# A list scheduler's order of 2,364 jobs replaced by one written plan, in a decoder trunk on one core

## The chip, the core and the metric

The kernel runs on one core of a Trainium2 chip. The metric is the device time of one execution in microseconds (us), as the median of several runs. One more execution was taken by the hardware profiler; all rows below come from that one.

## What is computed

One layer of a hybrid decoder trunk on 512 positions of width 1024, all in float32: a mixer with three branches, and a feed-forward part with a short convolution. `_causal_dwconv` is a convolution over positions, one filter for each channel; `y_c`, whose lines are left out, is attention with 4 heads to 256 memory rows.

```python
def _mixer(x, mem, ...):
    h = _rmsnorm(x, norm_mix_g)
    p_a, p_b, q, p_g = jnp.split(h @ w_in, IN_SPLITS, axis=-1)
    gb, gc, v = jnp.split(p_a, 3, axis=-1)
    y_a = (gb * _causal_dwconv(gc * v, conv_a_w)) @ w_a_out        # 3 taps
    u, ug = jnp.split(p_b, 2, axis=-1)
    u = _causal_dwconv(u * jax.nn.sigmoid(ug), conv_b_w) + conv_b_bias   # 31 taps
    y_b = jax.nn.silu(_layernorm(u, ln_b_g, ln_b_b)) @ w_b_out
    ...
    merged = g[:, :, 0] * y_a + g[:, :, 1] * y_b + g[:, :, 2] * y_c
    return merged @ w_o

def _conv_ffn(x, norm_ffn_g, w_up, conv_ffn_w, w_down):
    u = _causal_dwconv(_rmsnorm(x, norm_ffn_g) @ w_up, conv_ffn_w)   # 3 taps
    gt, up = jnp.split(u, 2, axis=-1)                                # 2 x 2816
    return (jax.nn.silu(gt) * up) @ w_down

# x = x + _mixer(...);  x = x + _conv_ffn(...);  out = _rmsnorm(x, norm_final_g)
```

## The kernel before, in words

**Products.** TensorE multiplies float32 in parts: every operand is split into a high part (an ACT cast, L649, `whi` for weights) and a low part (a DVE subtraction, L653, `wlo`), and each product is hi·hi, hi·lo and lo·hi. The large projections go further: four blocks of weights (2 x 2 blocks of 512 rows by 256 columns, 512 KB each) make a "quad" that is computed by seven products instead of eight, as in Strassen's method. A quad's products are named (quad, 1) to (quad, 7), for instance `(("up", 2), 6)`; each is 24 matmuls of 256 columns (`multiply`, L819). The operands that are sums of blocks are made in place by the DMA queue of POOL (GpSimd), which adds a block of weights onto a loaded tile (`more`, L773): for a quad q the jobs `("s5", q)`, `("s6", q)`, `("s7", q)`, `("s3", q)`. Plain loads of 512 KB go through SP's queue (L679): `("ld", (q, "u"))` and v, s, r. So a product in the feed-forward part hangs on a chain of load (SP), accumulate (POOL), cast `("wh", ...)` (ACT), subtraction `("wl", ...)` (DVE) and product (PE). The last projection (`pd`) and the merge use plain products of 512 or 256 columns (L600 to L602).

**Other work.** ACT and DVE read the products' banks (L864 and its neighbours on DVE, L848 to L885 on ACT), and DVE makes convolution taps (L1598), `z` = up times gate (L1969), its differences (`zs`, L606, and `zd`, L2170) and their low parts (`zl`, L2197). The last steps are sums of squares (`sr`, L2365), the root and the reciprocal (L2383, L2437), the scaling (`sa`, L2389, and `sv`, L2402) and the stores.

**What sets the order.** All work is put down as 2,364 jobs in the class `Jobs` (L244 to L467). A job has a name, an engine, a cost, a function that emits its instructions, the jobs that it comes after, the tiles that it takes and the tiles that it uses. A tile takes a slot of a ring: 17 `sb`, 6 `lf`, 8 banks of PSUM `ps`, 6 `wf` (the landing places of weights), 6 `tm`. `latest_starts` gives every job a due time from the order of the products and shifts it by a table for each kind of job (`LATER`); `run` then goes through a model of the machine, and again and again takes the job that can start first, by due time among equals, not earlier than `AHEAD` before its due time. It models the two DMA queues (`moved`, `transfer`, `SHARE`) and takes the slot that came free first. Each engine then executes its instructions in the order in which they were emitted. When the model lets a DMA of SP or POOL start later than its queue was free, `wait_for` makes it wait for the last instruction of PE, ACT or DVE that the model had ended by then:

```python
if start > free[e] + PACE and early:
    wait_for(self.tc, code[n_code], max(early, key=lambda d: d[0])[1])
```

The casts and subtractions write into a short ring of `whi` and `wlo` tiles: the cast for a product comes after the product `UNIT_BUFS` products earlier (in `split_job`).

Of the kernel before, what the change touches and what calls it, by code (L numbers as in the profile page):

```python
# [56 lines left out]
SOON = 8.0  # L57

SHARE = 0.39
# [18 lines left out]
LATER = {  # L78
    "ACT c3": -79.87, "ACT cf": -109.54, "ACT csq": -49.02, "ACT exp": -408.18,
# [3 lines left out]
    "ACT mg": -6.51, "ACT mgh a": -131.92, "ACT mgh b": -203.04, "ACT mgh c": -161.97,  # L83
    "ACT mgh d": -323.72, "ACT mgh e": -90.58, "ACT mgh f": 308.75, "ACT mgh g": -153.29,
    "ACT msq": 15.04, "ACT mu high": -0.01, "ACT oh": -226.41, "ACT pth": -176.82,
# [12 lines left out]
    "ACT table end": -197.25, "ACT table exp": 5.67, "ACT table gates": 1.59,  # L98
    "ACT table glu": -252.31, "ACT table last": -0.01, "ACT table silu": -28.73,
    "ACT table swish": -15.77, "ACT table v": -32.24, "ACT table x": -1.37, "ACT tap 0": -202.88,  # L100
    "ACT tap 1": 192.35, "ACT tap 2": 130.71, "ACT tap 3": 262.1, "ACT tp 0": 393.84,
# [9 lines left out]
    "ACT xroot": -17.08, "ACT xsq": 6.07, "ACT xsquare": -30.79, "ACT zh a": -613.81,  # L111
    "ACT zh b": -91.24, "ACT zh d": -69.92, "ACT zh e": -4.53, "ACT zh f": -126.12,
    "ACT zh g": -8.78, "DVE CV": -695.74, "DVE c3": -191.73, "DVE centre": 202.15,
    "DVE cf": 294.92, "DVE csum": -277.07, "DVE ends": -149.6, "DVE fl h b00": 0.11,
# [6 lines left out]
    "DVE low": 2.25, "DVE m fold": 28.63, "DVE m scale": 0.66, "DVE mg": -19.19,  # L121
    "DVE mgl a": -285.28, "DVE mgl b": 9.87, "DVE mgl c": 24.34, "DVE mgl d": -328.43,
# [111 lines left out]
def wait_for(tc, ins, other):  # L234
# [5 lines left out]
        reason="paced",  # L240
    )


class Jobs:  # L244

    def __init__(self, tc, rings):
# [2275 lines left out]
```

## Time and profile before

| | before |
|---|---|
| median of 3 runs | 895.22 us (895.15 to 895.43) |
| span of the profiled execution | 894.3 us |
| PE busy | 886.0 us, 99% of the span |
| DVE busy | 822.5 us, 92% |
| ACT busy | 677.8 us, 76% |
| POOL busy | 126.8 us, 14% |
| moved by DMA | 190.59 MB, 213 GB/s in the mean |

Times are in us from the start of the span; in a row of a timeline the first column is the start, the second the busy time, then engine, line, operation, output<-inputs, shapes, the number of instructions put together, and in brackets the idle time of the engine just before with what ended it. Matmuls overlap, so the distance from start to start says what one costs, not its busy time.

### The profile page before, as it was taken

What the parts mean: (1) busy time and instruction counts of PE and PEld (TensorE: products, weight loads), DVE (VectorE), ACT (ScalarE), POOL (GpSimd) and SP (SyncE); (2) the same over time, 40 slices, a digit from 0 to 9 for tenths busy, and PEclk for the clock granted to TensorE, in tenths of its full rate; (3) what the DMA queues carried; (4) which work ended last, traced back from release to release, by engine and by line L of the source; (5) the groups of instructions that cost most, each with busy time, mean ns of one, the idle gap of its engine ahead of it and who ended that gap; (6) DMA issues with size and microseconds to landing.
All of it is one profiled execution on the core that took longest, in us unless ns stands there. A gap on an engine that the chain in (4) does not pass through costs nothing.

```text
span 894.3 us, 16686 instructions
## 1 busy us (share of the span) xinstructions
PE 886.0 (99%) x6649; PEld 847.4 (95%) x6649; DVE 822.5 (92%) x928; ACT 677.8 (76%) x933; POOL 126.8 (14%) x153
## 2 busy tenths in 40 slices
PE   9999999999999999999999999999999999999997
PEld 8999999999989999999899988899999999998886
DVE  6997999999989999999897969898999889999997
ACT  7767989989987888787967753776766677875665
POOL 0021121111011121111100011021211121001220
PEclk9999999999999999999999999999999999999999
DMA  9999789767569997988856497499999877779992
GB/s 357 391 256 209 151 196 195 189 138 171 165 161 233 210 212 179 231 190 218 212 111 213 178 337 160 115 236 309 281 239 231 210 163 151 197 261 323 229 220 96
DMA packets 54221, 190.59 MB, mean 213 GB/s; under 512 B 6144, under 2 KB 6528, under 8 KB 54144
## 3 DMA queue, kind: packets, MB, share of 16 engines
q0 software_dynamic: 20880, 75.24, 47.0%
q1 hardware_dynamic: 32976, 114.02, 35.3%
q8 instruction: 52, 0.85, 0.4%
q10 hardware_dynamic: 288, 0.27, 0.1%
q14 instruction: 25, 0.20, 0.1%
HBM read 185.31 MB, written 4.19 MB: 212 GB/s over the span
## 4 chain that ended last, share of the span: by engine, by line
PE 93%; DVE 5%; issue 1%; ACT 0%; DVEq 0%
PE bank L819 57%; PE bank L601 6%; PE bank L602 6%; PE bank L600 6%; PE bank L1649 5%; PE bank L1651 5%; PE bank L1650 5%; PE bank L1153 2%; DVE wlo L653 2%; DVE zl L2197 1%; DVE upc L1598 1%; DVE gtc L1598 1%; PE bank L2014 0%; PE bank L1889 0%; PE bank L1393 0%
## 5 line engine op out<-in xcount | busy, mean ns | idle before, releaser
L653 DVE TENSOR_TENSOR wlo<-wf,whi 128x1024 fp32r<-128x1024 f32 x196 | 235.0, 1210 | 22.6 <-ACT whi L649 22.4
L649 ACT CAST whi<-wf 128x1024 fp32r<-128x1024 f32 x202 | 209.4, 1042 | 60.8 <-PE bank L819 18.8
L1465 ACT ACTIVATE tp<-u,pk 128x511 f32<-128x511 f32 (+22 forms) x184 | 118.8, 705 | 3.1 <-DVE acc L1472 2.5
L1472 DVE TENSOR_TENSOR acc<-acc,tp 128x1022 f32<-128x1022 f32 (+22 forms) x92 | 109.2, 1187 | 6.8 <-ACT tp L1465 5.1
L773 POOL DMA_DIRECT2D wf<-in_w_in x52 | 46.5, 914 | 231.8 <-DVE wlo L653 148.5
L819 PE MATMUL bank<-ft6h,wlo 128*128 128x256 f32 x232 | 64.0, 276 | 1.1 <-DVE wlo L653 1.1
L819 PE MATMUL bank<-fb10h,whi 128*128 128x256 f32 x232 | 64.0, 276 | 0.0
L819 PE MATMUL bank<-fb11h,whi 128*128 128x256 f32 x232 | 64.0, 276 | 0.0
L819 PE MATMUL bank<-ft5l,whi 128*128 128x256 f32 x232 | 63.9, 275 | 0.0
L819 PE MATMUL bank<-fb11h,wlo 128*128 128x256 f32 x232 | 63.9, 275 | 0.0
L819 PE MATMUL bank<-fb00h,whi 128*128 128x256 f32 x232 | 63.9, 275 | 0.0
L819 PE MATMUL bank<-fb00l,whi 128*128 128x256 f32 x232 | 63.9, 275 | 0.0
L819 PE MATMUL bank<-fb00h,wlo 128*128 128x256 f32 x232 | 63.8, 275 | 0.0
L819 PE MATMUL bank<-fb10l,whi 128*128 128x256 f32 x232 | 63.8, 275 | 0.0
L819 PE MATMUL bank<-fb10h,wlo 128*128 128x256 f32 x232 | 63.8, 275 | 0.0
L819 PE MATMUL bank<-ft5h,wlo 128*128 128x256 f32 x232 | 63.8, 275 | 0.0
L819 PE MATMUL bank<-ft6l,whi 128*128 128x256 f32 x232 | 63.8, 275 | 0.0
L819 PE MATMUL bank<-ft7l,whi 128*128 128x256 f32 x232 | 63.8, 275 | 0.0
L819 PE MATMUL bank<-ft7h,wlo 128*128 128x256 f32 x232 | 63.8, 275 | 0.0
L819 PE MATMUL bank<-ft4l,whi 128*128 128x256 f32 x232 | 63.8, 275 | 0.0
L819 PE MATMUL bank<-ft4h,wlo 128*128 128x256 f32 x232 | 63.8, 275 | 0.0
L819 PE MATMUL bank<-fb11l,whi 128*128 128x256 f32 x232 | 63.8, 275 | 0.0
(388 smaller groups left out, 3144.5 us busy)
## 6 DMA issues: line engine op xcount, KB each, us to landing
wf<-in_w_in SPq DMA_DIRECT2D x53, 512.0 KB, 5.2
wf<-in_w_in POOLq DMA_DIRECT2D x52, 512.0 KB, 7.0
wf<-in_w_up POOLq DMA_DIRECT2D x33, 512.0 KB, 8.3
wf<-in_w_up SPq DMA_DIRECT2D x30, 512.0 KB, 7.9
wf<-in_w_down SPq DMA_DIRECT2D x15, 512.0 KB, 4.4
wf<-in_w_att_out SPq DMA_DIRECT2D x8, 512.0 KB, 4.0
wf<-in_w_a_out SPq DMA_DIRECT2D x8, 512.0 KB, 4.4
wf<-in_w_b_out SPq DMA_DIRECT2D x8, 512.0 KB, 5.4
```

The source lines that it names most:

```text
L600: nc.tensor.matmul(ps, s_hi, w_hi, start=start, stop=False, skip_group_check=again)
L601: nc.tensor.matmul(ps, s_hi, w_lo, start=False, stop=False, skip_group_check=again)
L602: nc.tensor.matmul(ps, s_lo, w_hi, start=False, stop=stop, skip_group_check=again)
L649: nc.scalar.copy(parts[0], src())
L653: nc.vector.tensor_tensor(lo, src(), hi.bitcast(F32), op=ALU.subtract)
L773: nc.gpsimd.dma_start(out=tiles[key], in_=block(w, col[c], k), accum_op=ALU.add)
L819: nc.tensor.matmul(ps[:, c, :], w[:, i, at], in_turns(a[i]), start=first and n == 0, stop=i == 3 and n == 2, skip_group_check=again,)
L1465: nc.scalar.activation(two(("tp", p, s))[:, j, s:], two(("u", p))[:, j, : SEQ - s], AF.Copy, scale=weight(j),)
L1472: nc.vector.tensor_tensor(a, a, two(("tp", p, s))[:, :, s:], op=ALU.add)
L1649: nc.tensor.matmul(ps, w_hi[:, i, at], hi, start=first, stop=False)
L1650: nc.tensor.matmul(ps, w_hi[:, i, at], lo, start=False, stop=False)
L1651: nc.tensor.matmul(ps, w_lo[:, i, at], hi, start=False, stop=last)
```

## The change

The tables of offsets `LATER` and `AHEAD`, the due times, the model of the queues and the choice among ready jobs go. In their place stands a list `PLAN` with one entry for each of the 2,364 jobs: its key, the slots that it takes, and, for some SP and POOL jobs, the job whose last instruction its DMA waits for. `run` walks the list. One dependency is new, `("rb", t - 1, i)` ahead of `("rb", t, i)` for odd t, on ACT. The jobs and their instructions are the same.

```diff
-LATER = {
-    "ACT c3": -79.87, "ACT cf": -109.54, "ACT csq": -49.02, "ACT exp": -408.18,
...
+PLAN = [
+    (("mem tile", 0), "sb4"), (("ldm", 0, 0), ""), (("mem tile", 1), "sb14"),
...
+    (("low", ("ya", 1)), "sb5"), (("s5", ("bb", 1)), "", (("cv", 3), 1)), ((("cv", 2), 4), ""),
...
+    (("wh", (("up", 2), 6)), ""), ((("cf", 0, 1), 1, 2), ""), (("s7", ("up", 2)), ""),
+    (("wh", (("up", 1), 4)), ""), ((("up", 1), 7), ""), ((("cf", 0, 1), "done"), ""),
+    (("z", 0), ""), (("r5", ("up", 1)), "tm4"), (("wl", (("up", 2), 6)), ""),
...
+    (("ld", (("up", 3), "v")), "lf4", (("up", 2), 6)), ((("cf", 1, 1), 0), "tm0"),
...
+    (("ld", (("up", 5), "u")), "wf2", (("up", 3), 7)), (("wh", (("up", 5), 5)), ""),
...
+    (("zs", "c", 1), ""), (("r6", ("up", 10)), ""), (("wh", ("pd", "a", 1)), ""),
...
+    (("wl", (("up", 10), 3)), ""), ((("cf", 9, 1), 1, 2), ""),
...
+    (("wl", ("pd", "a", 4)), ""), (("wh", ("pd", "b", 3)), ""), (("xa", 1), ""),
+    (("zl", "a", 2), "lf3"), ((("cf", 10, 1), 1, 2), ""), (("yl", 0), ""), (("pd", "a", 4), ""),
+    (("zs", "d", 1), ""), (("wh", ("pd", "b", 4)), ""), (("silu", 10, 1), ""),
+    (("wl", ("pd", "b", 3)), ""), (("wh", ("pd", "a", 5)), ""), (("z", 10, 1), ""),
...
-    def run(self, log=None):
-        due, users = self.latest_starts()
...
+    def run(self):
+        done, last, left, holder = set(), {}, {}, {}
...
+        for key, given, *held in PLAN:
+            engine, fn, after, take, use = self.jobs[key]
...
+            fn()
             if len(code) > n_code:
...
+                for other in held:
+                    wait_for(self.tc, code[n_code], last[other])
+                last[key] = code[-1]
```

The order of before is not written in its source; it is what `run` gives. Set against it, engine by engine, at least so many jobs of each engine stand in another order in the plan (all others keep their order among themselves): 23 of 350 on PE, none of these by more than 4 places, 291 of 755 on ACT, 355 of 857 on DVE, 35 of 145 on POOL and 93 of 221 on SP. 525 of 668 tiles lie in another slot. 158 DMAs were held for an instruction of another engine before, 280 are in the plan; 3 of them for the same job.

## Rows read from the trace of the kernel before

**Rows 1.** The page: span, then each engine's busy us, share and instructions

```profile
span 894.3 us, 16686 instructions
PE 886.0 (99%) x6649; PEld 847.4 (95%) x6649; DVE 822.5 (92%) x928; ACT 677.8 (76%) x933; POOL 126.8 (14%) x153
```

**Rows 2.** All waits of PE: line waited for, us in total, times, longest

```profile
PE bank L819 <- DVE wlo L653: 1.1, 1, 1.1
PE bank L2014 <- DVE ones L2017: 1.1, 1, 1.1
PE bank L601 <- DVE wlo L653: 0.7, 1, 0.7
```

**Rows 3.** Timeline of PE around 620 us: start, busy us, instruction, [idle before]

```profile
620.23 0.28 PE L819 MATMUL bank<-ft6h,whi 128*128 128x256 f32 x1
620.34 0.28 PE L819 MATMUL bank<-ft6l,whi 128*128 128x256 f32 x1
621.69 0.38 PE L819 MATMUL bank<-ft6h,wlo 128*128 128x256 f32 x1 [1.07 <-DVE wlo L653]
```

**Rows 4.** Timeline of PE, 787 to 808 us

```profile
787.55 0.27 PE L819 MATMUL bank<-ft4h,whi 128*128 128x256 f32 x1
...
805.86 0.38 PE L600 MATMUL bank<-whi,zh 128*128 128x512 f32 x1
806.90 0.48 PE L601 MATMUL bank<-wlo,zh 128*128 128x512 f32 x1 [0.66 <-DVE wlo L653]
807.22 0.38 PE L602 MATMUL bank<-whi,zl 128*128 128x512 f32 x1
```

**Rows 5.** Timeline of ACT after the last matmul

```profile
888.82 0.39 ACT L2365 ACTIVATE j<-bank 128x256 f32<-128x256 f32 x1 [0.40 <-PE bank L602]
```

**Rows 6.** Timeline of DVE, 603 to 626 us

```profile
605.49 2.36 DVE L653 TENSOR_TENSOR wlo<-wf,whi 128x1024 fp32r<-128x1024 f32 x2 [1.52 <-ACT whi L649]
...
611.03 2.36 DVE L653 TENSOR_TENSOR wlo<-wf,whi 128x1024 fp32r<-128x1024 f32 x2 [0.82 <-ACT whi L649]
...
620.41 1.22 DVE L653 TENSOR_TENSOR wlo<-wf,whi 128x1024 fp32r<-128x1024 f32 x1
```

**Rows 7.** Timeline of ACT, 603 to 626 us

```profile
609.94 2.01 ACT L649 CAST whi<-wf 128x1024 fp32r<-128x1024 f32 x2 [1.91 <-DMA wf<-in_w_up]
```

**Rows 8.** DMA issues, 600 to 626 us: count, size, us from issue to landing

```profile
wf<-in_w_up POOLq DMA_DIRECT2D x4, 512.0 KB, 9.2
...
('up', 5)_966_7323<-in_w_up SPq DMA_DIRECT2D x1, 512.0 KB, 19.8
```

**Rows 9.** Timeline of DVE, 750 to 812 us

```profile
754.65 1.23 DVE L653 TENSOR_TENSOR wlo<-wf,whi 128x1024 fp32r<-128x1024 f32 x1 [1.46 <-ACT whi L649]
...
759.03 0.68 DVE L864 TENSOR_TENSOR gt<-gt,bank 128x512 f32<-128x512 f32 x1
759.63 1.22 DVE L653 TENSOR_TENSOR wlo<-wf,whi 128x1024 fp32r<-128x1024 f32 x1
760.76 0.75 DVE L1598 SCALAR_TENSOR_TENSOR upc<-uu,pk,upc 128x510 f32<-128x510 f32 x1
761.43 1.53 DVE L1598 SCALAR_TENSOR_TENSOR gtc<-gt,pk,gtc 128x511 f32<-128x511 f32 x2
762.88 1.22 DVE L653 TENSOR_TENSOR wlo<-wf,whi 128x1024 fp32r<-128x1024 f32 x1
...
805.63 1.22 DVE L653 TENSOR_TENSOR wlo<-wf,whi 128x1024 fp32r<-128x1024 f32 x1
```

**Rows 10.** DMA issues of the whole span, the two tiles of quad ('bb', 1)

```profile
('bb', 1)_526_3942<-in_w_in POOLq DMA_DIRECT2D x3, 512.0 KB, 8.3
...
('bb', 1)_553_4187<-in_w_in POOLq DMA_DIRECT2D x1, 512.0 KB, 11.4
```

**Rows 11.** Timeline of PE, 342 to 354 us

```profile
342.43 0.28 PE L819 MATMUL bank<-fb00h,wlo 128*128 128x256 f32 x1
...
353.26 0.28 PE L819 MATMUL bank<-ft5h,whi 128*128 128x256 f32 x1
```

More of the change, by code (lines that the diff above doesn't have):

```diff
@@ L253, in __init__ @@
         self.tc = tc
-        self.jobs, self.place, self.left = {}, {}, {}
-        self.rings = {r: {i: 0.0 for i in range(n)} for r, n in rings.items()}
-        self.at, self.work = 0.0, {"SP": 0.0, "POOL": 0.0}
-        self.written = set()
+        self.jobs, self.place, self.rings = {}, {}, rings
         self.first = []
@@ L261, in add @@
         assert key not in self.jobs, key
-        for name, *_ in take:
-            assert name not in self.left, name
-            self.left[name] = [0, 0.0]
-        names = [name for name, *_ in take] + list(use)
-        latency = latency or SEEN.get(engine, 0.0)
-        self.jobs[key] = (engine, cost, fn, list(after), latency, list(take), names)
-    def kind(self, key):
-        engine = self.jobs[key][0]
-        if engine == "SP" and key in self.first:
-            words = ("first",)
-        elif isinstance(key, str):
-            words = (key,)
-        elif key[0] in ("wh", "wl", "wn", "ld"):
-            unit = key[1][1] if key[1][0] == "raw" else key[1]
-            if isinstance(unit[0], tuple):
-                words = key[0], "up" if unit[0][0] == "up" else "mix", unit[1]
-            else:
-                words = key[0], unit[0], unit[1] if unit[0] in ("merge", "pd") else 0
-        elif key[0] in ("r1", "r2", "r3", "r4", "r5", "r6", "r7", "s3", "s5", "s6", "s7"):
-            words = key[0], key[1][0]
-        elif key[0] in ("tap", "tp", "sa", "sv", "sq", "hd", "sr", "rt", "rc"):
-            words = key[:2]
-        elif isinstance(key[0], tuple):
-            words = [w for w in key[0] if isinstance(w, str)]
-        else:
-            words = [key[0]] + [w for w in key[1:] if isinstance(w, str)]
-        return " ".join(str(w) for w in (engine, *words))
@@ L324, in partly @@
-    def partly(self, name):
-        return name[0] in ("ss", "rows") or name[1] in ("warm", "end")
-    def free_places(self, ring, leave=0):
-        ring, _, whole = ring.partition("=")
-        own, _, other = ring.partition("+")
-        own, other = (
-            [(at, r, i) for r in rs.split() for i, at in self.rings[r].items()
-             if not whole or i in self.written]
-            for rs in (own, other)
-        )
-        return sorted(own + (other if len(other) > leave else []), reverse=True)
@@ L340, in moved @@
-    def moved(self, queue, start):
-        share = SHARE if queue == "SP" else 1.0 - SHARE
-        mine, other = self.work[queue], self.work["POOL" if queue == "SP" else "SP"]
-        if other == 0.0:
-            return start + mine
-        both = min(mine / share, other / (1.0 - share))
-        return start + both + mine - both * share
-    def transfer(self, queue, start, cost):
-        work, t = self.work, self.at
-        share = {"SP": SHARE, "POOL": 1.0 - SHARE}
-        while t < start and (work["SP"] > 0.0 or work["POOL"] > 0.0):
-            both = work["SP"] > 0.0 and work["POOL"] > 0.0
-            rate = share if both else {"SP": 1.0, "POOL": 1.0}
-            step = min([start - t] + [work[q] / rate[q] for q in work if work[q] > 0.0])
-            for q in work:
-                work[q] -= rate[q] * step if work[q] > 0.0 else 0.0
-                if work[q] < 1e-9:
-                    work[q] = 0.0
-            t += step
-        self.at = start
-        work[queue] += cost
@@ new lines, in add, with places @@
+        self.jobs[key] = (engine, fn, list(after), list(take), list(use))
+    def places(self, key, given):
+        for (name, ring, *_), at in zip(self.jobs[key][3], given, strict=True):
+            r = at.rstrip("0123456789")
+            self.place[name] = r, int(at[len(r) :])
+            assert r in ring.replace("+", " ").split("=")[0].split(), (name, ring, at)
+            assert self.place[name][1] < self.rings[r], (name, at)
+            yield name
+    def run(self):
+        assert sorted(map(str, self.jobs)) == sorted(str(key) for key, *_ in PLAN)
+        done, last, left, holder = set(), {}, {}, {}
+        for _, _, _, take, use in self.jobs.values():
+            for name in [name for name, *_ in take] + use:
+                left[name] = left.get(name, 0) + 1
+        for key, given, *held in PLAN:
+            engine, fn, after, take, use = self.jobs[key]
+            assert done.issuperset(after), (key, [k for k in after if k not in done])
+            for name in self.places(key, given.split()):
+                assert not left.get(holder.get(self.place[name]), 0), (key, name)
+                holder[self.place[name]] = name
@@ L453, in run @@
-            ends[key] = free[e] + latency
-            for k in dict.fromkeys(users.get(key, ())):
-                waits[k] -= 1
-                ready_at[k] = max(ready_at.get(k, 0.0), ends[key])
-                if not waits[k] and self.jobs[k][0] != "PE":
-                    ready.setdefault(self.jobs[k][0], {})[k] = ready_at[k]
-            for name in names:
-                left = self.left[name]
-                left[0] -= 1
-                left[1] = max(left[1], ends[key])
-                if not left[0]:
-                    ring, i = self.place[name]
-                    self.rings[ring][i] = left[1]
@@ L466, in run @@
-            n -= 1
+                for other in held:
+                    wait_for(self.tc, code[n_code], last[other])
+                last[key] = code[-1]
+            for name in [name for name, *_ in take] + use:
+                left[name] -= 1
+            done.add(key)
 @with_exitstack
@@ L1942, in hybrid_block_kernel @@
             blk = ("h2b", i, r)
-            job(("rb", t, i), "ACT", actv(512), lambda t=t, i=i: row_block(t, i), [("tr", t)],
+            job(("rb", t, i), "ACT", actv(512), lambda t=t, i=i: row_block(t, i),
+                [("tr", t)] + ([("rb", t - 1, i)] if t % 2 else []),
                 use=[bank] + ([blk] if t % 2 else []), take=[] if t % 2 else [(blk, "lf")])
```

265 lines of the change are left out of this document (110 added, 155 removed), and 814 rows, old and new, of tables (AHEAD, LATER, PLAN).

## The prediction

> **What bounds the kernel now.** I read four views in this order. The page's first part says that PE is busy for 99% of the span [rows 1]: the order of jobs can give back only what PE loses. The list of PE's waits says where that is: three waits in 350 products [rows 2]. The timeline of PE at the two waits for `wlo` gives their price from start to start, since the ends of matmuls are modelled. At 620.34 the distance to the next start is 621.69 − 620.34 = 1.35 where the one before is 0.11, so this stall costs 1.24 us [rows 3]. At 805.86 it is 806.90 − 805.86 = 1.04 where 512 columns take twice 0.11, 0.22: 0.82. The matmul behind it starts after 0.32 instead of 0.22: another 0.10, so this stall costs 0.92 [rows 4]. The third wait, for `ones`, stands ahead of warming matmuls while the first loads come, and the first product waits for data, not for it: 0. Behind the last matmul stands a chain of 5.5 us (888.82 to 894.3) of sums, root, scaling and stores [rows 1, 5].
>
> So the most that a new order can take from PE is 1.24 + 0.92 = 2.16 us. The span is 894.3 [rows 1] and the median 895.22, so some 0.9 us lie outside the span and stay. The floor of this change is 895.22 − 2.16 = 893.06, and 0.2% is 1.79 us (893.43 to 897.01; about what a measurement of this kernel can tell from no change).
>
> **The change, part by part.** The instructions are the same, so nothing is added or removed on any engine; jobs move, and DMAs are held for other jobs.
>
> *The start and the end.* The first loads and products stand in the same order, and the last sums, root, reciprocal and scaling form the same chain. I give both 0, with bounds of 0.2 less and 0.2 more: that is half of the 0.40 that ACT waits for PE at the last sum [rows 5], the only slack that I find there.
>
> *Stall 1, product (up 2, 6).* Its `wlo` starts on DVE at 620.41 and ends at 621.63, while PE wanted it at 620.45 [rows 3, 6]. DVE has the same amount of work ahead of it in the plan. But in the 15 us before, DVE stood idle for 1.52 + 0.82 = 2.34 us, both times for a cast [rows 6], and the cast stood idle for the landing of an accumulated tile, 1.91 us at 609.94 [rows 7]. The accumulates of this stretch took 9.2 us to land, and a load that isn't needed for long took 19.8 [rows 8]: loads for quads 3 to 5 share the DMA engines with accumulates for quads 0 to 2. The plan changes just that. The SP loads of (up 3) v, (up 4) s and u and (up 5) u are held for later jobs or come later in the queue; `s7` of (up 2) goes behind `s5` of (up 3); and `wl` of (up 0, 6) is ahead of one or two other DVE jobs (1.9 us of work) so that `s3` of (up 0), which waits for it, is issued earlier. To close the stall, 1.24 of the 2.34 us must go. Bounds: nothing, if the accumulates land no sooner, and 1.24 (what is late next is then the product itself, on time). I take 1.24, since the two waits that made it are the ones whose DMA neighbours leave. Past POOL's queue: `s5` of (up 3) is one issue earlier and `s7` of (up 2) one later, which its product, five places on (13 us, against 9.2 to land and 2.2 for cast and subtraction), doesn't feel.
>
> *Stall 2, product (pd a, 4).* Here DVE has no idle time from 754.65 on [rows 9]: it is simply late by its own work. So I price its order by starts: an instruction of 1024 columns takes 1.14 (759.63 to 760.76, as the others), one of 512 0.60 (759.03 to 759.63), a tap 0.67 (760.76 to 761.43), and of two taps on one row of a tile the second costs 0.11 more (761.43 to 762.88 is 1.45) [rows 9]. Put on the order of before these prices give 805.83 for the `wlo` that PE waited for; it started at 805.63 [rows 9], so they are 0.2 too slow, the error that I allow below. The plan has 27 wide instructions, 6 of 512 columns and 23 taps, 2 of them behind a tap of the same row, between the same anchor and `zl` (a, 2), which now stands behind `wl` (pd a, 4): 27 × 1.14 + 6 × 0.60 + 23 × 0.67 + 2 × 0.11 = 30.78 + 3.60 + 15.41 + 0.22 = 50.01. So `wlo` starts at 754.65 + 50.01 − 1.14 = 803.52 and ends 1.22 later at 804.74, where PE wants it at 805.86 + 0.22 = 806.08; `zl` follows and ends at about 805.6, wanted at 806.3. The stall goes, with 0.7 us to spare: −0.92. Two moves do it: `wl` (pd b, 3) goes behind, and 9 pairs of dependent taps become 2; against them stands `zs` (c, 1), which is pulled ahead. What is late next is priced now.
>
> *Two new places.* The plan puts product (up 10, 3) ahead of (up 10, 4), two places sooner, at 787.55 where (up 10, 4) was [rows 4]; its first use of `wlo` is due at 787.55 + 0.22 = 787.77. Ahead of that `wl` stand 18 wide, 4 of 512, 13 taps, 1 pair: 20.52 + 2.40 + 8.71 + 0.11 = 31.74; it ends at 754.65 + 31.74 + 1.22 = 787.61, or 0.2 sooner: on time by 0.16 if the error holds its sign, 0.04 late if it turns. And `wl` (pd b, 3) stands behind `zl` (a, 2) (768 columns: 0.60 + half of 0.54 = 0.87), a tap and `zs` (d, 1): 804.66 + 0.87 + 0.67 + 1.14 + 1.22 = 808.56, where PE, after 12 matmuls of 0.22, wants it at 805.86 + 2.64 + 0.22 = 808.72. Both are within 0.2 of being late. Bounds for the two together: 0 to 0.6 (0.3 each, the error and a POOL or ACT hand-over of its size more); I take 0.2, nearer to the sums.
>
> *Held DMAs.* 280 DMAs instead of 158 are held for a job of another engine, and most loads come later. A DMA that is issued later costs nothing while it lands before its cast is due. The narrowest place that I find among the accumulates is `s5` of (bb 1): held for product (cv 3, 1), whose last matmul starts at 342.43 and is over at 342.7. Its cast and its subtraction come to 1.0 + 1.2 [rows 7, 9], and product (bb 1, 5) is due at 353.26, its first `wlo` at 353.49 [rows 11]; with 0.2 for the hand-overs the tile must land by about 351.1. That is a lead of 8.4 us. The POOL issues on the two tiles of (bb 1) landed after 8.3 in the middle, and one after 11.4 [rows 10]. Cost by these ends: below nothing is excluded, since PE has no wait there to lose; at 8.3 it is 0; at 11.4 it is 3.0. I take 0, the end at which three of the four issues have their middle, and keep the other end as a rival.
>
> On this step the Trainium skill speaks against the change: "DMA: Bandwidth & Descriptors", section "Rules for kernel authors", says that a DMA should be issued early and waited for late, with compute between. The rows say that early has a price here too: the load that was issued far ahead took 19.8 us and its neighbours 9.2 [rows 8]. By the rule the 122 added holds would cost and not save, which is case D below; by the row they clear the way for what is due next.
>
> **Sum.** 895.22 − 1.24 − 0.92 + 0.2 = 893.26, so 893.3 (span about 892.4).
>
> **The rivals.**
> A, the forecast, 0.55: both stalls close, new waits 0 to 0.6: 892.8 (the floor less 0.2 at start or end) to 893.9. For it: work ahead of stall 2 is counted, not guessed, and stall 1 has a spare of 1.1 us. Of the 0.55, 0.38 lie below 893.43, since the sum is only 0.15 under that line.
> B, 0.17: one of the two stalls stays (most likely stall 1, whose closing hangs on landings that I can't price), or a third wait of its size comes: 893.26 + 0.92 = 894.2 to 893.26 + 1.24 = 894.5; with its ends 893.9 to 895.2. For it: rows 7 show a wait for landing, and no row shows how fast an accumulate lands with fewer neighbours.
> C, 0.10: the plan does not do what it says: it is another order of the same quality, each stall closes here and opens there, 895.2. For it: DVE has 92% of the span [rows 1], so a stretch that is relieved loads another. Against it: two stalls in 350 products are few, and I found no new product with less than 0.2 us to spare but the two above.
> D, 0.18, the other side: late issues land late, at `s5` of (bb 1) for one. With its lead of 8.4 and a landing of 11.4 PE waits 3.0 there, and nothing behind gives it back, since PE is dense to the end: 893.3 + 3.0 = 896.3. It decides from a landing of 8.4: above 10.3 the gain of 1.9 is gone, above 12.1 the kernel is slower by over 0.2%, and at the 19.8 of rows 8 it would be 904.7. For it: 8.3 and 8.4 are the same number. Against it: with other loads held back too, the queue in front of `s5` is shorter than the one that gave 11.4. I put 0.12 over 897.01 and 0.06 below.
>
> **How the numbers follow.** The time is A's, 893.3. Faster by over 0.2% is A's part below 893.43: 0.38. Slower is D's part over 897.01: 0.12. Within 0.2% is the rest: 0.17 of A, B, C and 0.06 of D: 0.50. The range goes from A's lower end, 892.8, over B and C to D's nearer case with 0.3 for what else moves, 896.6: it leaves out D's 0.12 and a few hundredths of A.
>
> **What would show it.** Stall 1: the wait at (up 2, 6) is gone, DVE has under 1.1 us idle between 603 and 620, and accumulates of 600 to 626 land in less than 9.2. If the wait is there with DVE still idle for casts, the step on landings was wrong. Stall 2: the `wlo` of (pd a, 4) starts near 803.5 − 1.2 (the whole stretch comes earlier by stall 1). New places: waits of PE for `wlo` near 786.5 and 807.5, of 0.3 at most each. Held DMAs: a wait of PE in the middle of the mixer, with an idle cast behind it that a DMA ended, would be case D; if PE has new waits of more than 1 us anywhere, my search for narrow places failed.

## The result, and the profile after

The changed kernel takes 898.6 us (897.21 to 899.09, 5 runs) where before takes 895.24 (895.15 to 896.04): ratio 1.0032, 95% interval 1.002 to 1.0045. On another chip it was 897.92 against 895.44, 1.0029 (1.0021 to 1.0038; run h1 below). So it is slower by 2.5 to 3.4 us; I had forecast 893.3 and a range up to 896.6.

The page's first part after, beside [rows 1]; the profiled execution took 897.85 us:

```profile
span 896.1 us, 16702 instructions
PE 886.8 (99%) x6649; PEld 847.3 (95%) x6649; DVE 820.7 (92%) x928; ACT 673.8 (75%) x933; POOL 127.2 (14%) x153
```

PE's waits after, beside [rows 2] (line waited for, us in total, times, longest):

```profile
PE bank L1348 <- DVE wlo L1182: 1.9, 3, 0.9
PE bank L2544 <- DVE ones L2547: 1.1, 1, 1.1
PE bank L1348 <- ACT gt L1377: 0.4, 1, 0.4
```

L1348 is the quads' `multiply` (L819 before), L1182 the subtraction (L653), L1178 its cast (L649). The wait of the last projection (L601 before, [rows 4]) is gone. The quads have three waits for `wlo` where [rows 2] had one, and one for a bank that ACT had not read. Two products carry nearly all of it, (up 1, 6) and (up 2, 6). Timeline of PE, answering [rows 3]:

```profile
612.88 0.28 PE L1348 MATMUL bank<-ft6l,whi 128*128 128x256 f32 x1
613.93 0.38 PE L1348 MATMUL bank<-ft6h,wlo 128*128 128x256 f32 x1 [0.77 <-DVE wlo L1182]
...
621.74 0.28 PE L1348 MATMUL bank<-ft7h,wlo 128*128 128x256 f32 x1
622.37 0.38 PE L1348 MATMUL bank<-ft6h,whi 128*128 128x256 f32 x1 [0.36 <-ACT gt L1377]
622.59 0.28 PE L1348 MATMUL bank<-ft6l,whi 128*128 128x256 f32 x1
623.77 0.38 PE L1348 MATMUL bank<-ft6h,wlo 128*128 128x256 f32 x1 [0.92 <-DVE wlo L1182]
```

And at (pd a, 4), answering [rows 4], and ACT behind the last matmul, answering [rows 5]:

```profile
807.96 0.38 PE L1129 MATMUL bank<-whi,zh 128*128 128x512 f32 x1
808.17 0.38 PE L1130 MATMUL bank<-wlo,zh 128*128 128x512 f32 x1
...
890.35 0.38 ACT L2895 ACTIVATE j<-bank 128x256 f32<-128x256 f32 x1 [0.64 <-PE bank L1131]
```

There the distance is 0.21: no stall. At the quads, from start to start, less 0.11: 0.94 at (up 1, 6), a new stall, and 0.52 + 1.07 at (up 2, 6), where before lost 1.24. The same products, start against start in the two profiled executions, give the balance of the spans:

| stretch | PE later by |
|---|---|
| up to the end of the mixer (565 us); 0.38 of it is a wait at (bb 1, 6), 369.6 us | +0.83 |
| 565 to 599 | −0.18 |
| (up 1, 6), with the wait of 0.94 | +0.96 |
| (up 2, 6) against its old wait | +0.49 |
| stall 2, (pd a, 4), gone | −0.93 |
| 876 us to the last matmul | +0.36 |
| behind the last matmul | +0.18 |
| span, 896.05 − 894.34 | +1.71 |

The medians of this group differ by more, 3.4 us: the profiled execution of before lies some 0.9 over its median (the base, the first point of the reasons below), and that of the changed kernel, 897.85, lies 0.75 under its own.

Why (up 1, 6) waits. DVE after, beside [rows 6], then ACT, beside [rows 7]: the subtractions wait for casts, the casts for accumulates, and longer than before.

```profile
609.87 1.23 DVE L1182 TENSOR_TENSOR wlo<-wf,whi 128x1024 fp32r<-128x1024 f32 x1 [1.62 <-ACT whi L1178]
612.65 1.23 DVE L1182 TENSOR_TENSOR wlo<-wf,whi 128x1024 fp32r<-128x1024 f32 x1 [1.55 <-ACT whi L1178]
```

```profile
608.77 1.06 ACT L1178 CAST whi<-wf 128x1024 fp32r<-128x1024 f32 x1 [2.07 <-DMA wf<-in_w_up]
611.57 1.99 ACT L1178 CAST whi<-wf 128x1024 fp32r<-128x1024 f32 x2 [1.73 <-DMA wf<-in_w_up]
```

DVE's idle time is 1.62 + 1.55 = 3.17 us where it was 2.34. The two casts wait for `s5` of (up 2) and `s6` of (up 1). What is issued beside them, timelines of SP and POOL after:

```profile
599.34 0.33 SPq L1208 DMA_DIRECT2D wf<-in_w_up  x1
599.77 0.48 SPq L1208 DMA_DIRECT2D ('up', 3)_939_7077<-in_w_up  x1
606.54 0.33 SPq L1208 DMA_DIRECT2D wf<-in_w_up  x1
```

```profile
599.34 0.86 POOL L1302 DMA_DIRECT2D wf<-in_w_up  x1 [2.87 <-DMA wf<-in_w_up]
601.90 0.86 POOL L1302 DMA_DIRECT2D wf<-in_w_up  x1 [1.70 <-DVE wlo L1182]
```

Issues from 600 to 626 us, answering [rows 8] (count, size, us to landing in the middle):

```profile
wf<-in_w_up POOLq DMA_DIRECT2D x6, 512.0 KB, 7.6
```

The accumulates of the stretch land after 7.6 us in the middle, where it was 9.2, but the two that decide do not: `s5` of (up 2) lands at 608.67, after 9.3 us, and `s6` of (up 1), issued at 601.90, at 611.49, after 9.6. In before these two took 9.4 and 9.1, but they were issued 1.9 and 1.1 us earlier, with PE only 0.65 earlier: part of the lateness is the later issue. The second row of SP is a load of quad (up 3), its tile s. The plan issues it at 599.77, unheld and between the two accumulates, though its own accumulate goes out only at 614.9; before issued it at 605.42. That is the suspect the experiments start from.

Why (up 2, 6) waits as well. From the start of the subtraction of (up 1, 6) to that of (up 2, 6), DVE works without a pause of note. Before, the distance is 620.41 − 611.03 = 9.38 us [rows 6]; after, it is 622.50 − 612.65 = 9.85, with a read of a bank in between that the plan puts behind the first subtraction and before has ahead of it (`r3` of (up 0)):

```profile
613.79 0.68 DVE L1393 TENSOR_TENSOR gt<-gt,bank 128x512 f32<-128x512 f32 x1
...
622.50 2.35 DVE L1182 TENSOR_TENSOR wlo<-wf,whi 128x1024 fp32r<-128x1024 f32 x2
```

The read takes 0.60 from start to start, and the taps, in another order, give back 0.12. Of the nineteen profiles here, the kernels below included, the eleven with DVE's order of before in this stretch have 9.4 us each, and the eight with the plan's 9.9. So once a late landing makes the first subtraction hold up PE, DVE's own work makes PE wait at (up 2, 6) again, in the plan 0.5 us longer.

### The profile page after: what moved, and what is told of

Its sections match the earlier page's. It is cut to its first block, busy times and chain, and to the rows that moved or that the text cites. A ratio compares the mean times of both kernels' runs of the same rounds, so it can differ in the third digit from the quotient of the medians.

```text
span 896.1 us, 16702 instructions
## 1 busy us (share of the span) xinstructions
PE 886.8 (99%) x6649; PEld 847.3 (95%) x6649; DVE 820.7 (92%) x928; ACT 673.8 (75%) x933; POOL 127.2 (14%) x153
## 4 chain that ended last, share of the span: by engine, by line
PE 81%; DMA 9%; DVE 4%; issue 3%; ACT 2%; SPq 0%; POOL 0%; DVEq 0%; POOLq 0%; ACTq 0%
PE bank L1348 52%; PE bank L2180 5%; PE bank L2178 5%; PE bank L2179 5%; PE bank L1129 4%; PE bank L1130 4%; PE bank L1131 4%; DMA wf<-in_w_up 3%; DMA wf<-in_w_in 2%; DVE wlo L1182 2%; PE bank L1682 2%; DMA x_sum<-in_w_down 2%; DMA wf<-in_w_down 2%; ACT whi L1178 1%; DMA wf<-in_w_v 1%
## 5 line engine op out<-in xcount | busy, mean ns | idle before, releaser
L1178 ACT CAST whi<-wf 128x1024 fp32r<-128x1024 f32 (+1 forms) x204 | 210.4, 1042 | 59.1 <-PE bank L1348 11.2
L1182 DVE TENSOR_TENSOR wlo<-wf,whi 128x1024 fp32r<-128x1024 f32 x198 | 237.2, 1211 | 15.8 <-ACT whi L1178 15.2
L1994 ACT ACTIVATE tp<-u,pk 128x507 f32<-128x507 f32 (+22 forms) x184 | 119.4, 704 | 5.3 <-DVE acc L2001 2.7
L1302 POOL DMA_DIRECT2D wf<-in_w_in x56 | 50.7, 964 | 271.6 <-DVE wlo L1182 88.7
L1348 PE MATMUL bank<-ft6h,wlo 128*128 128x256 f32 x232 | 64.1, 276 | 1.9 <-DVE wlo L1182 1.9
L1348 PE MATMUL bank<-ft6h,whi 128*128 128x256 f32 x232 | 64.2, 277 | 0.4 <-ACT gt L1377 0.4
L1348 PE MATMUL bank<-fb11h,whi 128*128 128x256 f32 x232 | 64.0, 276 | 0.0
L1348 PE MATMUL bank<-fb10h,whi 128*128 128x256 f32 x232 | 63.9, 275 | 0.0
L1348 PE MATMUL bank<-ft7h,whi 128*128 128x256 f32 x232 | 63.9, 275 | 0.0
L1348 PE MATMUL bank<-fb00h,whi 128*128 128x256 f32 x232 | 63.9, 275 | 0.0
L1348 PE MATMUL bank<-ft4h,whi 128*128 128x256 f32 x232 | 63.9, 275 | 0.0
L1348 PE MATMUL bank<-ft5l,whi 128*128 128x256 f32 x232 | 63.8, 275 | 0.0
L1348 PE MATMUL bank<-fb11h,wlo 128*128 128x256 f32 x232 | 63.8, 275 | 0.0
L1348 PE MATMUL bank<-fb10h,wlo 128*128 128x256 f32 x232 | 63.8, 275 | 0.0
L1348 PE MATMUL bank<-fb00l,whi 128*128 128x256 f32 x232 | 63.8, 275 | 0.0
L1348 PE MATMUL bank<-fb00h,wlo 128*128 128x256 f32 x232 | 63.8, 275 | 0.0
L1348 PE MATMUL bank<-fb10l,whi 128*128 128x256 f32 x232 | 63.8, 275 | 0.0
L1348 PE MATMUL bank<-ft5h,wlo 128*128 128x256 f32 x232 | 63.8, 275 | 0.0
L1348 PE MATMUL bank<-ft6l,whi 128*128 128x256 f32 x232 | 63.8, 275 | 0.0
L1348 PE MATMUL bank<-ft7l,whi 128*128 128x256 f32 x232 | 63.8, 275 | 0.0
L1348 PE MATMUL bank<-ft7h,wlo 128*128 128x256 f32 x232 | 63.8, 275 | 0.0
```

Source lines behind the costliest of these rows:

```text
L1178: nc.scalar.copy(parts[0], src())
L1182: nc.vector.tensor_tensor(lo, src(), hi.bitcast(F32), op=ALU.subtract)
L1302: nc.gpsimd.dma_start(out=tiles[key], in_=block(w, col[c], k), accum_op=ALU.add)
L1348: nc.tensor.matmul(ps[:, c, :], w[:, i, at], in_turns(a[i]), start=first and n == 0, stop=i == 3 and n == 2, skip_group_check=again,)
L1994: nc.scalar.activation(two(("tp", p, s))[:, j, s:], two(("u", p))[:, j, : SEQ - s], AF.Copy, scale=weight(j),)
```

## The experiments

In short: the early load, taken out of the plan's way or given to before, moves the time by about 2 us in either direction; in the plan without holds the same move is worth 0.5, within the noise. The holds and the written form of the plan do not make the loss. What remains with the load out of the way, 0.7 to 2 us, is not traced to one place.

All kernels run the changed kernel's code; only entries of `PLAN` differ. The cuts show entries of the plan, each with its job, its slots and the job that it is held for; the line breaks are not those of the source. Each group ran beside before on one chip; the times are medians.

| run | what | us | before | ratio, 95% interval |
|---|---|---|---|---|
| e1 | order of before as a plan | 895.58 | 895.59 | 1.0001 (0.9992 to 1.001) |
| e2 | plan, no holds | 897.86 | 895.59 | 1.0024 (1.0015 to 1.0033) |
| e3 | plan, load s of (up 3) held | 896.28 | 895.59 | 1.0006 (0.9997 to 1.0015) |
| e4 | plan, `s7` (up 1) behind `s5` | 899.16 | 895.59 | 1.004 (1.0026 to 1.0053) |
| f1 | before, one subtraction moved | 895.27 | 895.27 | 0.9996 (0.9987 to 1.0005) |
| f2 | f1, four loads held | 903.15 | 895.27 | 1.0077 (1.0064 to 1.0091) |
| f3 | before, load s of (up 3) early | 897.78 | 895.27 | 1.0022 (1.0013 to 1.0031) |
| f4 | e3, `s3` (cv 3) earlier | 902.0 | 895.27 | 1.0078 (1.0065 to 1.0092) |
| g1 | before to 753 us, then plan | 896.39 | 895.31 | 1.001 (1.0001 to 1.0019) |
| g2 | plan to 570 us, then before | 896.02 | 895.31 | 1.0008 (0.9999 to 1.0017) |
| g3 | g1, two loads held late | 895.7 | 895.31 | 1.0005 (0.9996 to 1.0014) |
| g4 | before to 567 us, then e3 | 897.36 | 895.31 | 1.0018 (1.0009 to 1.0028) |
| h1 | the changed kernel again | 897.92 | 895.44 | 1.0029 (1.0021 to 1.0038) |
| h2 | the kernel of g1 again | 896.63 | 895.44 | one run |
| h3 | g1, no holds after 753 us | 895.98 | 895.44 | 1.0006 (0.9997 to 1.0014) |
| h4 | plan, only that load held | 897.22 | 895.44 | 1.0021 (1.001 to 1.0032) |
| i1 | before, two loads held late | 895.39 | 895.49 | 0.9998 (0.9989 to 1.0007) |

**Is it the order, or the written plan?** e1:

```diff
-    (("mem tile", 0), "sb4"), (("ldm", 0, 0), ""), (("mem tile", 1), "sb14"),
...
+    (("mem tile", 0), "lf0"), (("mem tile", 1), "lf1"), (("ldm", 0, 0), ""),
...
```

> The changed kernel's code, with the order of before written out as its plan (same jobs, slots and holds as before). If the loss lies in the new order: 895.2 us, PE waits only at the two places of before (1.24 and 0.92 us), and as much time outside the span as before has. If the written plan itself costs (the time outside the span is 1.8 us in the changed kernel's profile, where I had reckoned 0.9 for before): about 896.1 with the same waits of PE.

895.58 beside 895.59, with the waits of before (0.42 at (up 1, 6) besides). The written plan costs nothing; the loss is in the order. The time outside the span is 1.7 to 1.9 us in every execution of every kernel here, before too, except h3, where it is 2.2 to 2.3.

**Are the holds too late?** e2:

```diff
-    (("s5", ("up", 2)), "", ("fh", "h2", "t5")),
+    (("s5", ("up", 2)), ""),
...
```

> The new plan with all 280 holds of SP and POOL DMAs taken away; order and slots as in the plan. If the holds make the late landings (my case D): the waits of PE at products (up 1, 6) and (up 2, 6), 0.94 and 0.53 + 1.08 us, get smaller, 896 us or less. If the accumulates land late because other transfers run beside them: without holds loads come earlier still and crowd more, so the same waits or longer ones, 898.6 to 903.

897.86. The waits are there as before the edit: 0.94 at (up 1, 6), 0.53 and 1.08 at (up 2, 6). The holds don't make them: case D, as I put it, falls. (One more wait of 0.83 us, at 832, stands in this profile and not in the plan's.)

**The one load, taken out of the plan's order and put into that of before.** e3 and f3:

```diff
-    ((("up", 0), 7), ""), (("ld", (("up", 3), "s")), "lf3"), (("wh", (("up", 0), 4)), ""),
-    (("wl", (("up", 0), 3)), ""),
+    ((("up", 0), 7), ""), (("wh", (("up", 0), 4)), ""),
+    (("wl", (("up", 0), 3)), ""), (("ld", (("up", 3), "s")), "lf3", ("wl", (("up", 0), 3))),
```

> The new plan with one load held longer: s of quad (up 3), which the plan issues at 599.8 us, is held for the subtraction of (up 0, 3) (end near 606.5) and put behind it. If this load is what slows the accumulates s5 of (up 2) and s6 of (up 1) (8.98 and 9.23 us to landing beside it): they land about 2 us sooner, the wait of PE at (up 1, 6) (0.94) goes and the one at (up 2, 6) shrinks by 0.5 or more: 896.0 to 897.6. If the accumulates are late because they are issued late or queue behind each other: no change, 898.6.

> The reverse of e3: the order of before, with the one load s of (up 3) issued at about 599 us, as in the new plan, where before issues it at 605.4 (its slot is exchanged with that of another tile). If this load ahead of its time is what costs the new plan 2.3 us: s5 of (up 2) and s6 of (up 1) land about 2 us later than in before, waits of 1 us or more at (up 1, 6) and (up 2, 6), 896.6 to 898. If it takes the rest of the new plan's order as well: 895.6.

The cut is e3's. f3 does the reverse in the order of before: it puts this load ahead of three others in SP's queue and lets it and one of them change slots.

e3 is 896.28, 0.7 over before instead of 2.5 to 3.4: this load's time is worth about 2 us. f3 is 897.78 against 895.27: the load, 6 us earlier, makes the order of before 2.5 us slower. Its profiled execution, 1.9 over that of before, has 0.14 + 0.94 at (up 1, 6) that before's has not, the same 1.24 at (up 2, 6), and some 0.9 of waits at 79 and 505 us, far from the load. The other 0.6 no profile places. Issues from 598.9 to 603.0 us, in the plan and then in e3 (queue, count, size, us to landing):

```profile
wf<-in_w_up POOLq DMA_DIRECT2D x2, 512.0 KB, 9.5
wf<-in_w_up SPq DMA_DIRECT2D x1, 512.0 KB, 4.6
('up', 3)_939_7077<-in_w_up SPq DMA_DIRECT2D x1, 512.0 KB, 9.3
```

```profile
wf<-in_w_up POOLq DMA_DIRECT2D x2, 512.0 KB, 7.2
wf<-in_w_up SPq DMA_DIRECT2D x1, 512.0 KB, 5.5
```

The same two accumulates land after 9.5 us in the middle beside the load and after 7.2 without it. The view gives 9.3 and 9.6 one by one for what the expectation has as 8.98 and 9.23. All these are single executions: without holds the pair takes 9.0 beside the load (e2) and 8.3 without (h4), and in the order of before 9.2 beside it (f3) and 7.8 to 9.3 without (six profiles). There the medians show the effect, not this pair's landings. DVE's idle time ahead of the second subtraction falls from 1.55 to 0.72:

```profile
610.72 1.23 DVE L1197 TENSOR_TENSOR wlo<-wf,whi 128x1024 fp32r<-128x1024 f32 x1 [0.72 <-ACT whi L1193]
```

In e3 PE has no wait at (up 1, 6) and 0.46 at (up 2, 6): 0.94 + 0.52 + 1.07 − 0.46 = 2.07 us less; the medians, each against its before, differ by 1.8 to 2.7.

**The queue of POOL.** e4:

```diff
-    (("s7", ("up", 1)), "", ("tr", 2)),
...
     (("s5", ("up", 1)), ""),
+    (("s7", ("up", 1)), "", ("tr", 2)),
```

> The new plan with one accumulate moved: s7 of (up 1) goes behind s5 of (up 1) in POOL's queue. If accumulates are late because they queue behind each other at some 3 us each: s5 of (up 1) lands some 2.5 us sooner (898.9 to 896.4 in the trace's time of 598.9 to 596.4); the wait at (up 1, 6) shrinks by up to 0.9 if that one lands in time for the subtraction to go sooner, 897.7; if DVE's order holds that subtraction anyway, no change, 898.6.

899.16, with the waits at the two quads as in the plan (0.19 + 0.94, 0.53 + 1.08). The order of these two is not it.

**Stall 2 by itself.** f1 moves one job of before:

```diff
-    (("wl", ("pd", "b", 3)), ""),
...
     (("wl", ("pd", "a", 4)), ""),
+    (("wl", ("pd", "b", 3)), ""),
```

> The order of before as a plan, with one job moved: the subtraction for product (pd b, 3) goes behind the one for (pd a, 4) on DVE. If that subtraction standing ahead makes the wait at (pd a, 4): the wait's 0.92 us go and nothing new comes (the subtraction of (pd b, 3) ends near 806.9, wanted at 808.7): 894.7 us where before has 895.6. If the work only moves the wait to another product: 895.6.

The wait at (pd a, 4) shrinks from 0.92 to 0.13, and the time stays: 895.27 in both. Timeline of PE in f1, 25 to 30 us later:

```profile
831.35 0.38 PE L1120 MATMUL bank<-whi,zh 128*128 128x512 f32 x1
831.82 0.48 PE L1121 MATMUL bank<-wlo,zh 128*128 128x512 f32 x1
832.14 0.38 PE L1122 MATMUL bank<-whi,zl 128*128 128x512 f32 x1
...
836.89 0.38 PE L1120 MATMUL bank<-whi,zh 128*128 128x512 f32 x1
837.50 0.48 PE L1121 MATMUL bank<-wlo,zh 128*128 128x512 f32 x1 [0.23 <-DVE wlo L1173]
837.82 0.38 PE L1122 MATMUL bank<-whi,zl 128*128 128x512 f32 x1
```

0.47 − 0.22 and 0.61 − 0.22, with 0.10 behind each: 0.84 us, which before doesn't have there. PE, no longer held at 806, runs into DVE at 831. DVE has no pause of more than 0.15 us from 805 to 840 in f1: its own work sets that stretch, and one order hands the loss to another product.

**The plan's end.** g1 and h2 (the same kernel) have the entries of before ahead of `("s3", ("up", 9))` and those of the plan from there on; h3 drops the 44 holds of that second part besides, as here:

```diff
-    (("ld", ("a", 3)), "wf5", (("cf", 9, 1), 0, 2)),
+    (("ld", ("a", 3)), "wf5"),
...
```

> The order of before up to 753 us (where the same jobs are done in both orders) and the new plan's order from there on. If the plan's end is better by the wait at (pd a, 4), as I forecast (0.92 us), and gives back only what its profile shows near 876 us and behind the last matmul (0.35 + 0.17): 0.4 us faster than before, 894.9 where before has 895.3; by my forecast without giving back, 894.4. If DVE's work alone limits the end, so that each order loses the same somewhere: 895.3.

> One more look at the kernel of g1 (order of before up to 753 us, the plan's from there), whose profile at 895.65 lies under its median of 896.39. If the end's loss is in the waits of PE after 753: a wait of half a us or more there, which the first profile lacks. If it is in the stores after the last matmul: no wait there, and over 6.0 us from the last matmul to the end.

> As g1, without the 44 holds of SP and POOL DMAs after 753 us. If loads held back to just before their use make the plan's end slow and uneven (g1: 896.4, from 894.6 to 897.6): 895.3 or less, and closer together. If the order of DVE and ACT there does: 896.4 as g1. If unheld loads crowd the accumulates of the end: more than g1.

g1 is slower than before by 1.1 us, not faster. Both its profiles show no PE wait of half a us after 753 us, so PE does gain stall 2 there. Part goes behind the last matmul: from its start to the end of the span it is 6.49 and 6.78 us in g1 and h2, 5.84 in before, 6.01 in both profiles of the changed kernel. That is 0.65 and 0.94 of the 0.92. Scaling and stores of earlier rows come later in the plan, just ahead of the last ones. SP's stores at the end, in the changed kernel:

```profile
890.53 0.89 SPq L2928 DMA_DIRECT2D out<-x  x2
891.90 0.83 SPq L2936 DMA_DIRECT2D out<-x  x2
...
out<-x SPq DMA_DIRECT2D x2, 128.0 KB, 2.5
out<-x ACTq DMA_DIRECT2D x1, 256.0 KB, 2.6
```

In before the last store of the earlier rows goes out at 888.73, where the last matmul starts at 888.51, and the last stores land after 2.0 and 2.1 us. The rest of g1's 1.1 us, and why its runs spread from 894.6 to 897.6, no profile showed. h3 (895.98) doesn't part from g1: without the holds the stores cost less (6.02) but PE waits 1.2 us at 829. Its median span, 893.8, is 0.8 under g1's and level with before's (893.7); 0.4 of that goes outside the span, and no run shows why. What the holds of the end cost stays open.

**Stall 1 in the order of before.** f2 moves four loads of before behind `("wl", (("up", 2), 6))`, v of (up 3), u and v of (up 4) and u of (up 5), and holds them for it; g3 and i1 only the two that are not needed for 30 us, behind s of (up 5):

```diff
-    (("ld", (("up", 4), "v")), "lf4"),
...
+    (("ld", (("up", 4), "v")), "lf4", ("wl", (("up", 2), 3))),
```

> As f1, and the four SP loads v of (up 3), u and v of (up 4) and u of (up 5), which before issues at 604.4 to 608.8 us, are held for the subtraction of (up 2, 6) and stand behind it in SP's queue. If loads beside the accumulates make the wait at (up 2, 6): it goes (1.24 us in the profiled execution of before, some 0.3 less than half in a typical one, whose span is 0.9 shorter), 893.4 to 894.4. If the accumulates are slow for another reason, or the held loads come too late for quads 3 to 5: 894.7 or more.

> As g1, and only the two loads of before that are not needed for 30 us and more (v of (up 4), u of (up 5), issued at 607 and 609 us) are held for the subtraction of (up 2, 3), 637 us, behind the next quad's loads. If those two crowd the accumulates of 600 to 620 us, and holding four at once in f2 only made a new crowd at 620: the waits at (up 1, 6) and (up 2, 6) shrink below 0.6 in all and no wait of 4 us comes: 894.0 to 894.7. If any load held there is missed later: 896 or more.

> The order of before as a plan, with the two loads of g3 alone held back (v of (up 4), u of (up 5), behind the subtraction of (up 2, 3) at 637 us); the end as in before. If these two loads crowd the accumulates of 600 to 620 us: the wait at (up 2, 6) falls from 1.2 to about 0.5 as in g3, the wait at (pd a, 4) stays 0.92, 894.6 where before has 895.3. If other work sets that time: 895.3.

In all three the wait at (up 2, 6) is about half of 1.23 (0.51, 0.45, 0.51). That alone shows little: with the order of before there untouched it was 1.23 in before, e1 and f1, 1.09 and 1.14 in g1 and h2, but 0.51 in g2 and h3. What is left is DVE's own: in f2, g2, g3, h3 and i1 the subtraction of (up 1, 6) doesn't wait for its cast; it stands behind `r3` of (up 0), which waits for PE, and starts 1.87 us ahead of its product; the 9.4 us of DVE's work to the next one then leave 0.45 to 0.52. So in these profiles of the order of before earlier landings are worth some 0.7 of the 1.24, not all of it. And f2 is 7.9 us slower. The four loads go out together at 620 us and now stand ahead of a load that is needed, r of (up 2). ACT's cast for it starts at 634.60 after 5.73 us of idle time, DVE stands 5.53 behind that, and the DVE read that PE needs ends at 640.08, though the view names a cast. The load's landing, PE's wait, and the granted clock behind it (window, busy us of PE and PEld, DVE, ACT, POOL, clock, DMA share, GB/s):

```profile
wf<-in_w_up SPq DMA_DIRECT2D x1, 512.0 KB, 12.2
```

```profile
636.28 0.28 PE L1342 MATMUL bank<-fb00h,wlo 128*128 128x256 f32 x1
640.23 0.55 PE L1342 MATMUL bank<-ft4h,whi 128*128 128x256 f32 x1 [3.67 <-ACT whi L1172]
```

```profile
630.00:636.00 6.00, 6.00 (x56) 6.00 (x55) 0.47 (x2) 1.40 (x2) 0.00 (x0) 1.00 1.04 328
...
642.00:644.00 2.00, 2.00 (x12) 2.00 (x11) 2.00 (x4) 1.06 (x1) 0.00 (x0) 0.50 1.06 234
...
646.00:648.00 2.00, 2.00 (x20) 2.00 (x20) 1.70 (x2) 2.00 (x4) 0.16 (x1) 1.00 1.03 356
```

That is case D, made by hand: 3.84 us of wait, and then TensorE at half its clock (0.50, so 1.2 of 2.4 GHz) until about 645.6, some 2.5 us more.

i1, with half of stall 1 gone and nothing else, is 895.39 against 895.49. The 0.7 us that I expected lie within its interval (±0.8), as no change does. Whether these two loads make stall 1, and what it is worth alone, is open; no kernel here is measurably under before.

**How thin the plan's margins are.** f4:

```diff
     (("wl", (("cv", 3), 6)), ""),
+    (("s3", ("cv", 3)), ""),
...
-    (("s3", ("cv", 3)), "", ("tp", 3, 1)),
```

> As e3 (the new plan with the load s of (up 3) held), and the accumulate s3 of (cv 3) put ahead of s6 of (bb 1) on POOL, without its hold, as in before. If its late landing makes the wait of 0.39 us at (bb 1, 6): that wait goes and 895.9 us are left where e3 had 896.3. If not, 896.3 with the wait still there.

The wait at (bb 1, 6) goes, and another comes at (cv 3, 4), 364.66 − 360.46 − 0.11 = 4.09 us:

```profile
364.66 0.55 PE L1364 MATMUL bank<-ft4h,whi 128*128 128x256 f32 x1 [3.92 <-ACT bank L1397]
```

ACT stands at a cast that waits for the load r of (cv 3). Issued at 350.45 in f4 and 351.77 in the plan, it took, in f4 and then in the plan:

```profile
wf<-in_w_in SPq DMA_DIRECT2D x1, 512.0 KB, 10.4
```

```profile
wf<-in_w_in SPq DMA_DIRECT2D x1, 512.0 KB, 4.5
```

One accumulate 7 us earlier (347.4 instead of 354.3) more than doubles the landing of a load that the plan holds to within a few us of its use; in e3, which lacks only this edit, the load took 5.1. Before issued it at 325.45.

**The mixer and the feed-forward part.** g2 and g4 join the orders at 570 and 567 us:

> The reverse cut: the new plan's order up to 570 us (mixer and output projection), the order of before from there on. If the plan loses some 0.6 to 0.8 us in the mixer (its profile shows PE later by 0.84 us at 565, 0.38 of it in one wait at (bb 1, 6)): 895.9 to 896.1. If the mixer's loss is only that execution's: 895.3.

> The order of before up to 567 us, and from there the new plan with the load s of (up 3) held as in e3. If e3 is still over before because of the mixer's order: e3's 0.7 us go, 895.3 to 895.6 less the plan's end, 894.9 to 895.3. If the feed-forward part of the plan loses them: 896.

g2 is 0.7 over before, as expected, but its profile has waits at the seam (568 to 574 us) that neither order has, 1.7 us in all, and none at (bb 1, 6): it shows nothing of the mixer. In g4 the waits at (up 2, 6) come back (0.30 + 1.08), with three of 0.3 to 0.7 from 650 to 773 us: 897.36, 2 us over before although the load is held. So e3's rest is not shown to be the mixer's, and holding the load is not the whole cure: with it held, (up 1, 6) has no wait in e3, f4 and g4 and 0.40 in h4, but (up 2, 6) has 0.46 and 0.63 in e3 and f4 and 1.4 and 1.6 in g4 and h4.

**What repeats, and the other holds.** h1 is the changed kernel unchanged; h4 is e2 with the entry of e3:

```diff
+    (("ld", (("up", 3), "s")), "lf3", ("wl", (("up", 0), 3))),
```

> The changed kernel once more, beside the three others of this group, on one chip: 898.2 to 898.7 where before has 895.3. A second profile of the same program shows which of its waits come every time: if late landings make those of (up 1, 6) and (up 2, 6), their sizes move by some tenths (0.94 and 0.53 + 1.08 in the first); waits that DVE's own work makes would repeat to 0.02.

> The new plan with no hold but one: the load s of (up 3) is held as in e3. If that load's time is the one that matters and the other 280 holds cost or bring little: e3's 896.3, less up to the 0.7 by which no_holds (897.9) lay under the changed kernel: 895.6 to 896.3. If the holds keep loads out of the way in the rest: 897 or more.

h1: 0.24 + 0.94 at (up 1, 6), 0.53 + 1.08 at (up 2, 6); the wait at (bb 1, 6) is absent, as is that at 876 us. The 0.53 + 1.08 repeat to 0.01 in the plan, h1, e2, e4 and h4. By what I had put down for h1 that means DVE's work and not landings, and DVE's 9.86 us between the two subtractions are that work; what moves by some tenths is the start of the wait at (up 1, 6). The 0.94 there repeats too, in f1 and f3 as well: when the cast comes last, PE still waits for one subtraction behind it.

h4 is 1.8 over its before, e2 2.3 and e3 0.7 over theirs. So without the holds the load's time is worth 0.5 us, and the intervals overlap. That the other holds help the second stall, as the prediction had it, fits the 0.53 + 1.08 of h4 beside the 0.46 of e3, but the intervals of these two overlap as well, and g4 has a like stall with holds: it is not shown.

## Why the prediction was wrong, step by step

**The base.** I took 0.9 us outside the span, from the median less the span. It is 1.8: the profiled execution of before took about 896.1 (its span, 894.3, and 1.8), 0.9 more than the median. Subtracting its stalls from a median that lies 0.9 lower put the floor 0.9 too low; against its own time it is 896.1 − 2.16 = 894.0. The executions of one order differ: with the order of before up to 753 us the wait at (up 1, 6) was 0 in before, g1, h2 and h3, 0.42 in e1 and 0.94 in f1, and that at (up 2, 6) 0.51 to 1.23.

**Stall 1, the step that failed.** "I take 1.24, since the two waits that made it are the ones whose DMA neighbours leave." I listed the loads that leave, and not the one that comes: s of (up 3), which the plan issues 5.7 us sooner, into just the two accumulates whose landing I was costing. The mechanism I named (loads beside accumulates) is what decides at (up 1, 6); its sign at this place was wrong. The landings go with it: `s6` of (up 1) lands at 611.0 to 611.7 in the five profiled executions with the early load (plan, h1, e2, e4, f3), each with a wait of 0.94 at (up 1, 6), and at 607.8 to 610.9 in the twelve others in which it is issued later and PE isn't moved by longer waits ahead (all but f4 and g2), nine of them without a wait there (h4 and e1 have 0.4, f1 0.94).

The second half of the step fails on DVE. "DVE has the same amount of work ahead of it in the plan" is wrong by 0.5 us: 9.86 between the two subtractions instead of 9.38. And the bound of 1.24, "what is late next is then the product itself, on time", is wrong too: DVE's own work leaves 0.45 to 0.52 of this stall in the order of before even where the cast is in time. The term of −1.24 measured +1.45, the sum of the two rows in the balance: 2.7 of the 3.7 us by which the span, 896.05, misses the 892.4 that I forecast. The rest is the 0.65 up to 599 us and the 0.54 from 876 us on, less the 0.2 of the new places.

**Stall 2.** The place was right: in g1 `wl` of (pd a, 4) starts at 803.05, where I had 803.52, and PE goes through. The size was wrong, since I took the wait for the gain. "What is late next is priced now" covered the next two products and not the next 30 us, in which DVE is dense (f1), nor the stores.

**The two new places.** Right: no wait at (up 10, 3) or (pd b, 3). In g1, where PE is not late, `wl` of (pd b, 3) ends at 808.07, and the product's first matmul starts at 808.08. The 0.2 that I took was 0.

**Start and end, 0 ± 0.2.** 0.18 behind the last matmul in the plan is within that; 0.65 and 0.94 in g1 and h2 are not. I had compared the last chain and not the stores of the rows ahead of it.

**Held DMAs.** `s5` of (bb 1) landed after 6.8 us, within its lead of 8.4 (beside [rows 10, 11]):

```profile
('bb', 1)_544_4113<-in_w_in POOLq DMA_DIRECT2D x1, 512.0 KB, 6.8
```

So D's place was wrong, and e2 shows that the holds aren't the cause. Landings got shorter in the plan, as the row on crowding let expect: 7.7 us in the mean of all 145 accumulates instead of 8.3, 5.6 instead of 6.9 for the 221 of SP that are not stores. What I missed is that one place with a longer landing decides. D's mechanism is real where holds bunch loads (f2) or an accumulate comes in front of a late load (f4).

By the Trainium skill's rule in "DMA: Bandwidth & Descriptors", section "Rules for kernel authors", a DMA is issued early. f3 is a case against it: this load issued 6 us earlier costs 2.5 us. f2 is a case for it: four loads held for 13 to 16 us, and the one behind them with them, cost 7.9. f4 is one for issuing a load early and against issuing an accumulate early beside it.

**The rivals.** What happened is none of them as written: the part of the plan's loss that is traced, about 2 us, is a load too early, where D had one too late. My 0.12 for slower by over 0.2% hung on one place of one kind; "I found no new product with less than 0.2 us to spare" rested on work counted on DVE and ACT, and (up 1, 6) and (bb 1, 6) hang on landings.

## What to carry to other kernels

When an order changes, list for every accumulate or load that PE will wait for what is newly issued beside it, from all queues; the loads that come count as much as those that leave. Count anew, too, what the feeding engine does between the last operand that came in time and the one that is late: here half a us had moved into that stretch. A wait in a stretch where the feeding engine is dense is worth little: look as far on as that engine stays dense before booking it as a gain. Take the base from the profiled execution's own total, and count small stalls from more than one execution.

## What the runs showed of the hardware

- Two accumulates of 512 KB landed 2.3 us sooner (7.2 instead of 9.5) when one load of 512 KB was issued 7 us later, in one profiled execution each; without holds it was 0.7 sooner (8.3 in h4 instead of 9.0 in e2).
- Behind a wait of 3.84 us (f2) the granted clock was 0.50 for some 5 us, so that the wait cost about 6.3 in all; f4's of 4.09 was followed by 0.50 as well. Waits of about 1 us, as at (up 1, 6) and (up 2, 6), left it at 1.00.
- One and the same program spread by 1.9 us (e1, 11 runs, 894.99 to 896.84), by 3.4 (before, 23 runs beside f1 to f4, 894.65 to 898.09) and by 3.2 (h1, 11 runs, 896.19 to 899.41).
